# Context's feed-forward in a hybrid retention trunk: from a planned loop to a list of units in a fixed order

## The chip, the cores and the metric

The kernel runs on one core of one Trainium2 chip. The metric is device time in microseconds (us) for one execution. The core has five instruction queues: TensorE (PE, matmuls; its weight loads are listed as PEld), VectorE (DVE), ScalarE (ACT), GpSimd (POOL) and SyncE (SP), which here issues nearly all DMAs. Each queue runs its instructions in order.

## The reference

One layer of a diffusion backbone: 1024 latent tokens and 256 context tokens of width 1024 pass through the same weights. Cut to what matters here:

```python
def swiglu(h, w1, w3, w2):
    return (jax.nn.silu(h @ w1) * (h @ w3)) @ w2

x = x + 0.5 * m_l[2] * swiglu(modulate(rms_norm(x, norm1_w), m_l[0], m_l[1]), ffn1_w1, ffn1_w3, ffn1_w2)
ctx = ctx + 0.5 * m_c[2] * swiglu(modulate(rms_norm(ctx, norm1_w), m_c[0], m_c[1]), ffn1_w1, ffn1_w3, ffn1_w2)
y_l, _ = token_mixing(modulate(rms_norm(x, norm2_w), m_l[3], m_l[4]),
                      modulate(rms_norm(ctx, norm2_w), m_c[3], m_c[4]), w_in, ...)
x = x + m_l[5] * y_l
x = x + 0.5 * m_l[8] * swiglu(modulate(rms_norm(x, norm3_w), m_l[6], m_l[7]), ffn2_w1, ffn2_w3, ffn2_w2)
return rms_norm(x, final_norm_w)
```

The hidden width is 2816, that is 22 blocks of 128 (f = 0 to 21). The change concerns the second of these lines: the first feed-forward, for the 256 context tokens.

## The kernel before

Everything is float32, and activations lie transposed: 128 features on the partitions, tokens along the free axis. A product of two float32 matrices is made of three fast matmuls (mm3, L63). Each operand is split (L58) into a high part, a rounded copy made by ACT, and a low part, the remainder, made by a subtraction on DVE or POOL. A weight block of 128 x 1024 is loaded and split as two halves of 128 x 512.

Token groups are numbered 0 and 1 (512 latent tokens each) and 2 (the context). The latent feed-forward is arranged as seven block products in place of eight (chain, L302, for w1 and w3; back6, L493, and prod, L466, for w2). back6 works off products 1, 2, 6, 5, 7 and 3, each in eleven pairs p; product 4 follows later. After each pair a feeder (L550) runs what stands at that place of `plan`, a table from the pair's number to small tasks: loads, steps of norms and the like. Products keep four PSUM banks "psa" or four "psb"; there are eight banks in all.

After back6 comes the context's feed-forward (L1575):

```python
for f in range(0, NF, 2):
    self.classic(f, (2,), mid2=(lambda: self.Y(f - 2, CT)) if f else None, ...)
    pend.pop(0)()
```

`classic` (L621) loads and splits w1 and w3 for blocks f and f+1, the low parts on POOL. H (L616) multiplies one weight block with the normed context into a psa bank: 24 matmuls of 256 columns. s1 (L578) takes the SiLU on ACT. s3 (L584) multiplies on DVE and splits the result into ghi (ACT) and glo (DVE). Y (L591) then multiplies the blocks f-2 and f-1 with w2: for each of the eight 128-row pieces m of the output, six matmuls into a fresh psb bank, and one DVE instruction (L600) that adds the scaled sum onto x. So x is updated 88 times over the eleven pairs. The last Y (f = 20) stands in `plan` after the second pair of product 4.

Between the pairs, `pend` runs the second norm of latent group 1 step by step: the rest of the sum of squares (norm2(1, 0), ahead of the loop), the row factor (L181, L197), eight steps norm_k (L226: two DVE instructions, one on ACT), and the spill of x to HBM. Then follow product 4, the norm of group 0, the context's key and value projections (ctx_k, ctx_v), mix_setup with lg_setup (L840: log-sigmoid of eight decay values by a row of tiny DVE instructions and one POOL power), and the mixing stage.

The order on each engine is set by a planner. It takes instructions by program order, moved by priorities: loading and splitting of weights are put 150 places ahead (WPRI), or, where POOL makes the low part, at their own place (WOFF). Raw loads use six buffers "raw" (NR), splits six pairs "whi"/"wlo" (NH), or slots of the activations' tiles that are free at the time (hslot). A block under `manual_schedule` keeps program order on the engines that it names; other work may still be put between. back6 is in such a block for SP alone. The context's loop is in none.

Of the kernel before, what the change touches and what calls it, by code (L numbers as in the profile page):

```python
# [31 lines left out]
class Trunk:  # L32
# [224 lines left out]
    def raw_half(self, src=None):  # L257
        t = self.tile(self.wp, [P, 512], F32, "raw", NR)
        if src is not None:
            t = t[:, :src.shape[1]]  # L260
            self.nc.sync.dma_start(t, src)
        return t
# [7 lines left out]
    def load_half(self, src, dst=None, eng=None):  # L270
        with self.tc.high_priority(offset=WOFF if eng else WPRI):
            return self.half(self.raw_half(src), dst, eng)

    def halves_slots(self, i):
        if i < 2:
            return None, None
        return tuple(self.hslot(f"0{2 * (i % 4) + j}") for j in range(2))

    def load_halves(self, src, dst=(None, None), eng=None):
        return [self.load_half(src[:, 512 * i:512 * i + 512], dst[i], eng) for i in range(2)]  # L280
# [310 lines left out]
    def Y(self, f, order, after=None, qs=(0, 1)):  # L591
# [18 lines left out]
        if after:  # L610
            for tg, o, n in order:
                for m in range(KD):
                    unit(ws[m // 4], tg, o, n, m)
                after(tg, o, n)

    def H(self, w, tg):  # L616
        ps = self.psA()
        self.proj(w, tg, ps)
        return ps
# [217 lines left out]
            act(a, a, AF.Exp, scale=-1.0)  # L837
            act(a, a, AF.Ln, bias=1.0)

    def lg_setup(self):  # L840
        nc, I, cp = self.nc, self.I, self.cp2
        x = self.tile(cp, [P, 8], F32, "lgx")
        nc.sync.dma_start(x, I["decay"].broadcast_to([P, 8]))
        e = self.tile(cp, [P, 8], F32, "lge")
        nc.vector.memset(e, float(np.e))
        u = self.tile(cp, [P, 8], F32, "lgu")
        nc.vector.tensor_scalar(out=u, in0=x, scalar1=-1.0, scalar2=None, op0=ALU.mult)
        nc.vector.tensor_tensor(out=u, in0=u, in1=x, op=ALU.min)
        nc.gpsimd.tensor_tensor(out=u, in0=e, in1=u, op=ALU.pow)
# [11 lines left out]
        nc.vector.scalar_tensor_tensor(out=x, in0=e, scalar=-2.0, in1=x, op0=ALU.mult, op1=ALU.add)  # L861
        self.lg = x
# [581 lines left out]
    def run(self):  # L1444
        nc, tc, I = self.nc, self.tc, self.I
        S = {}

        def opn(name, side="left"):
            S[name] = tc.tile_pool(name=name, bufs=1, reuse_waits="tile", side=side)
            return S[name].__enter__()  # L1450

        def cls(name):
            S[name].__exit__(None, None, None)
# [19 lines left out]
        with tc.manual_schedule(engines={mybir.EngineType.PE, mybir.EngineType.DVE, mybir.EngineType.Activation}):  # L1473
            ws = self.first1((xp, xp, None), n1)
# [24 lines left out]
        hc = opn("hc", "right")  # L1499
        self.gp = hc  # L1500
        n2 = opn("n2", "right")
        self.alloc_h((2,), hc)
# [32 lines left out]
        norm2 = lambda tg, i: norm_step(tg, i, self.mcol(4, int(tg == 2)), self.mcol(3, int(tg == 2)))  # L1535
        for i, at in enumerate((24, 27, 30, *range(33, 33 + KD))):
            plan[at].append(lambda i=i: ctx1(i))

        CT = [(2, 0, 256)]
        p4 = 6 * NP  # L1540
        plan[p4 + 1] += [lambda: self.Y(NF - 2, CT), lambda: self.alloc_h((2,), hc), lambda: norm2(2, 0)]
        plan[p4 + 4].append(lambda: norm2(2, 1))
        plan[p4 + 6].append(lambda: norm2(2, 2))
        for k in range(KD):
# [27 lines left out]
        self.alloc_h((1,), self.hp)  # L1572
        norm2(1, 0)
        pend = [lambda i=i: norm2(1, i) for i in range(1, 3 + KD)] + [lambda: spill(1)]
        for f in range(0, NF, 2):  # L1575
            self.classic(f, (2,), mid2=(lambda: self.Y(f - 2, CT)) if f else None, eng=[nc.gpsimd if e else None for e in CENG])
            pend.pop(0)()
        A = self.bank4(self.psA)
        self.prod(4, A, True)
        self.add4(0, 1, A)  # L1580
# [7 lines left out]
            norm2(0, 3 + k)  # L1588
        spill(0)
        cls("n2"), cls("hc"), cls("xp")  # L1590
        self.cp2 = opn("cp2", "right")
        self.mix_setup()
        cls("f1")
# [52 lines left out]
NLOW = 150  # L1646
SH = 2
NR = 6
EMODS = ((5, (0,)), (2, (0, 1)), (1, (1,)), (0, (1,)), (4, (0, 1)), (3, (0, 1)), (7, (0,)), (6, (0,)))
MPER = 6  # L1650
NH = 6
# [14 lines left out]
CENG = (1, 1, 1, 1)  # L1666
# [98 lines left out]
```

## Time and profile before

| | us |
|---|---|
| median of 3 runs | 2174.63 (2174.54 to 2177.96) |
| profiled execution | 2173.67 |
| span of its trace, first to last instruction | 2171.8 |
| PE busy | 2113.6 (97%) |
| DVE busy | 1525.9 (70%) |
| ACT busy | 979.9 (45%) |
| POOL busy | 279.9 (13%) |

Times in the trace count from the first instruction. A row of a group names the line, the engine, the operation, output and inputs, their shapes and the count, then busy time and mean duration, then the idle time of that engine just ahead of those instructions and who ended it. A line may be that of a helper: L60 and L61 are the two halves of every split, L65 to L67 the three matmuls of every mm3. A matmul's listed duration is longer than the distance to the next one, since matmuls overlap; the distance between starts is its cost. In rows of stretches the two numbers after the granted clock are the busy share of the DMA engines and GB/s.

### The profile page before, as it was taken

How to read it: one execution, taken by the hardware profiler on the slowest of the kernel's cores; microseconds unless marked ns; L12 is line 12 of the kernel's file. 1: busy time of each engine (PE TensorE's matmuls, PEld its weight loads, DVE VectorE, ACT ScalarE, POOL GpSimd, SP SyncE). 2: the span in 40 equal slices, each digit the busy share in tenths (PEclk: the TensorE clock that was granted, in tenths of full speed). 3: DMA queues.
4: the chain of work that ended last, by engine and by line, in shares of the span. 5: the costliest groups of instructions: out<-in, count | busy, mean ns of one | idle time of the engine just before them, and what ended most of it. 6: DMA issues, size and time to landing. Idle time of an engine off the chain costs nothing. (4 is left out here: it accounts for less than half of the span.)

```text
span 2171.8 us, 32819 instructions
## 1 busy us (share of the span) xinstructions
PE 2113.6 (97%) x11558; PEld 1806.7 (83%) x11558; DVE 1525.9 (70%) x2735; ACT 979.9 (45%) x1811; POOL 279.9 (13%) x285
## 2 busy tenths in 40 slices
PE   8999999999999899999989999999999999999998
PEld 7888888888889899987778987787878888888888
DVE  7889999756766756844666556858777666665686
ACT  4434334345545444547455335524343433434553
POOL 0000000000025662611132113200000000010000
PEclk9999999999999999999999999999999999999999
DMA  9267768569966565653322322324144444467674
GB/s 332 83 232 242 268 222 272 168 221 328 305 201 191 161 183 172 179 155 103 94 67 62 99 55 90 121 93 155 61 129 160 139 157 160 155 213 248 212 243 146
DMA packets 202933, 373.39 MB, mean 172 GB/s; under 512 B 24016, under 2 KB 37264, under 8 KB 202768
## 3 DMA queue, kind: packets, MB, share of 16 engines
q1 hardware_dynamic: 202336, 371.16, 52.9%
q8 instruction: 90, 1.47, 0.3%
q14 instruction: 75, 0.61, 0.1%
q10 hardware_dynamic: 432, 0.13, 0.0%
HBM read 296.72 MB, written 66.09 MB: 167 GB/s over the span
## 5 line engine op out<-in xcount | busy, mean ns | idle before, releaser
L60 ACT ACTIVATE whi<-raw 128x512 fp32r<-128x512 f32 (+1 forms) x563 | 346.9, 622 | 615.7 <-PE psa L66 181.1
L61 DVE TENSOR_TENSOR wlo<-raw,whi 128x512 fp32r<-128x512 f32 (+1 forms) x533 | 369.3, 696 | 309.0 <-ACT whi L60 304.6
L65 PE MATMUL psa<-hh,whi 128*128 128x512 f32 (+1 forms) x1108 | 434.4, 392 | 0.1
L66 PE MATMUL psa<-hl,whi 128*128 128x512 f32 (+1 forms) x1108 | 433.8, 391 | 0.0
L67 PE MATMUL psa<-hh,wlo 128*128 128x512 f32 (+1 forms) x1108 | 433.5, 391 | 0.0
L65 PE MATMUL psb<-hh,whi 128*128 128x512 f32 (+1 forms) x680 | 259.8, 382 | 0.5 <-ACT whi L60 0.5
L67 PE MATMUL psb<-hh,wlo 128*128 128x512 f32 (+1 forms) x680 | 259.7, 382 | 0.6 <-DVE wlo L61 0.6
L66 PE MATMUL psb<-hl,whi 128*128 128x512 f32 (+1 forms) x680 | 259.5, 382 | 0.0
L65 PEld LDWEIGHTS psa<-hh,whi 128*128 128x128 f32 x1108 | 208.7, 188 | 42.1 <-ACT s L314 0.6
L67 PEld LDWEIGHTS psa<-hh,wlo 128*128 128x128 f32 x1108 | 208.6, 188 | 41.6
L66 PEld LDWEIGHTS psa<-hl,whi 128*128 128x128 f32 x1108 | 208.6, 188 | 40.9
L67 PEld LDWEIGHTS psb<-hh,wlo 128*128 128x128 f32 x680 | 127.8, 188 | 25.8 <-DVE wlo L61 1.0
L65 PEld LDWEIGHTS psb<-hh,whi 128*128 128x128 f32 x680 | 127.9, 188 | 25.4 <-ACT whi L60 1.0
L66 PEld LDWEIGHTS psb<-hl,whi 128*128 128x128 f32 x680 | 127.9, 188 | 24.6
L60 ACT ACTIVATE hh<-raw 128x512 fp32r<-128x512 f32 x180 | 110.3, 622 | 72.6 <-PE psa L66 38.2
L61 POOL TENSOR_TENSOR hl<-raw,hh 128x512 fp32r<-128x512 f32 x84 | 117.5, 1410 | 67.2 <-ACT hh L60 62.6
L1095 POOL TENSOR_TENSOR nr<-nr,mhalf 128x4 f32<-128x4 f32 (+1 forms) x11 | 10.6, 963 | 867.5 <-DVE nr L1094 867.5
L65 PE MATMUL psa<-hh,hh 128*128 128x256 f32 x376 | 107.5, 286 | 1.2 <-DVE s L587 1.2
L67 PE MATMUL psa<-hh,hl 128*128 128x256 f32 x376 | 107.5, 286 | 0.0
L66 PE MATMUL psa<-hl,hh 128*128 128x256 f32 x376 | 107.4, 286 | 0.0
L65 PE MATMUL psa<-whi,hh 128*128 128x256 f32 (+1 forms) x320 | 93.3, 292 | 1.2 <-ACT s L1049 1.2
L66 PE MATMUL psa<-wlo,hh 128*128 128x256 f32 (+1 forms) x320 | 93.2, 291 | 1.0 <-DVE wlo L61 0.9
(402 smaller groups left out, 4238.2 us busy)
## 6 DMA issues: line engine op xcount, KB each, us to landing
raw<-in_w SPq DMA_DIRECT2D x374, 256.0 KB, 3.2
gd<-s SPq DMA_DIRECT2D x154, 256.0 KB, 2.8
ada<-in_adaT SPq DMA_DIRECT2D x76, 512.0 KB, 4.8
raw<-gd SPq DMA_DIRECT2D x91, 256.0 KB, 3.4
s<-in_w SPq DMA_DIRECT2D x66, 256.0 KB, 4.7
sd<-s SPq DMA_DIRECT2D x44, 256.0 KB, 3.1
raw<-sd SPq DMA_DIRECT2D x44, 256.0 KB, 2.9
hh<-in_w SPq DMA_DIRECT2D x44, 256.0 KB, 3.9
```

Of the source, the lines that this page charges most:

```text
L60: nc.scalar.activation(hi, src, AF.Copy)
L61: (eng or nc.vector).tensor_tensor(out=lo, in0=src, in1=hi.bitcast(F32), op=ALU.subtract)
L65: mm(ps, wa[0], xa[0], start=start, stop=False, skip_group_check=more)
L66: mm(ps, wa[0], xa[1], start=False, stop=False, skip_group_check=more)
L67: mm(ps, wa[1], xa[0], start=False, stop=stop, skip_group_check=more)
L1095: nc.gpsimd.tensor_tensor(out=r, in0=r, in1=self.mhalf[:, :n], op=ALU.pow)
```

## The change

The loop becomes a list of units: ("1", f) and ("3", f) for w1 and w3 of a block, ("y", f) for w2 of blocks f and f+1. The order is 1 0, 3 0, 1 1, 3 1, 1 2, 3 2, y 0, 1 3, 3 3, 1 4, 3 4, y 2 and so on. ctx_ffn walks the list under `manual_schedule` for all five queues. At each unit it issues the load of the unit five places on (CLA); at a "1" or "3" it also issues the split of the "1" or "3" two places on among these, and one of the four halves of the next y, then the matmuls, then s1 or s3. The w2 sums of all blocks stay in four psb banks, two pieces m to a bank, and x is updated eight times after the last y, which stands at the same place of `plan` as before.

Raw weights are loaded into the pool "s" (19 buffers, also used for the latent stream's kept sums) in place of "raw". The first five units are loaded after pairs 3 to 7 of product 3 and the first two split after pairs 8 and 9. The norm of group 1 takes its steps one by one behind the y units (its banks now psa, its four diagonal tiles made at once), and each of its result tiles is allocated when its step comes. lg_setup is cut in two: lg_start (the log-sigmoid) stands right behind the block, ahead of product 4.

```diff
+    def ctx_sums(self, f, ws):
+        for m in range(KD):
+            ps = self.yb[m // 2][:, m % 2 * CTX:(m % 2 + 1) * CTX]
+            for i in range(2):
+                self.mm3(ps, [t[:, m % 4 * P:(m % 4 + 1) * P] for t in ws[2 * (m // 4) + i]], self.g[f + i, 2],
+                         not (f or i or m % 2), f == NF - 2 and i == 1, True)
+            if f == NF - 2:
+                x = self.x[2][m]
+                self.nc.vector.scalar_tensor_tensor(out=x, in0=ps, scalar=self.gates_m[1][:, m:m + 1], in1=x,
+                                                    op0=ALU.mult, op1=ALU.add)
...
+    def ctx_load(self, u):
+        self.craw[u] = []
+        for src in self.ctx_src(u):
+            t = self.stile()
+            self.nc.sync.dma_start(t, src)
+            self.craw[u].append(t)
+        self.cw[u] = []
...
+    def ctx_hsplit(self, u):
+        j = 2 * u[1] + (u[0] == "3")
+        for i in range(2):
+            slot = f"1{(self.ng // 2 + 5 + 2 * j + i) % 8}" if j < 4 else f"0{2 * (j % 4) + i}"
+            self.ctx_split(u, self.hslot(slot), self.nc.gpsimd)
+
+    def ctx_ffn(self, units, norms):
+        self.yb = self.bank4(self.psB)
+        hs = [u for u in units if u[0] != "y"]
+        ys = [u for u in units if u[0] == "y"]
+        j = 0
+        for i, u in enumerate(units):
+            for v in units[i + CLA:i + CLA + 1]:
+                self.ctx_load(v)
+            if u[0] != "y":
+                j += 1
+                for v in hs[j + 1:j + 2]:
+                    self.ctx_hsplit(v)
+                for v in ys[:1]:
+                    if v in self.cw and len(self.cw[v]) < 4:
+                        self.ctx_split(v)
+                ps = self.H(self.cw.pop(u), 2)
+                (self.s1 if u[0] == "1" else self.s3)(u[1], 2, ps)
+            else:
+                self.ctx_sums(u[1], self.cw.pop(u))
+                ys.pop(0)
+                if norms:
+                    norms.pop(0)()
...
-        CT = [(2, 0, 256)]
         p4 = 6 * NP
-        plan[p4 + 1] += [lambda: self.Y(NF - 2, CT), lambda: self.alloc_h((2,), hc), lambda: norm2(2, 0)]
+        units = []
+        for f in range(0, NF, 2):
+            units += [("1", f), ("3", f)] + ([("y", f - 2)] if f else []) + [("1", f + 1), ("3", f + 1)]
+        self.craw, self.cw = {}, {}
+        for i in range(CLA):
+            plan[5 * NP + 3 + i].append(lambda u=units[i]: self.ctx_load(u))
+        for i in range(2):
+            plan[5 * NP + 8 + i].append(lambda u=units[i]: self.ctx_hsplit(u))
+        last = ("y", NF - 2)
+        plan[p4 + 1] += [lambda: self.ctx_sums(NF - 2, self.cw.pop(last)), lambda: self.alloc_h((2,), hc), lambda: norm2(2, 0)]
...
-        pend = [lambda i=i: norm2(1, i) for i in range(1, 3 + KD)] + [lambda: spill(1)]
-        for f in range(0, NF, 2):
-            self.classic(f, (2,), mid2=(lambda: self.Y(f - 2, CT)) if f else None, eng=[nc.gpsimd if e else None for e in CENG])
-            pend.pop(0)()
...
+        norms = [lambda: norm2(1, 1), diag1, rows1] + [lambda k=k: norm1(k) for k in range(KD - 1)]
+        with tc.manual_schedule(engines={mybir.EngineType.PE, mybir.EngineType.DVE, mybir.EngineType.Activation,
+                                         mybir.EngineType.Pool, mybir.EngineType.SP}):
+            self.ctx_ffn(units, norms)
+            self.ctx_load(last)
+        for _ in range(4):
+            self.ctx_split(last)
+        norm1(KD - 1)
+        spill(1)
+        self.lg_start(n2)
+        self.psN = self.psB
```

More of the change, by code (lines that the diff above doesn't have):

```diff
@@ L272, in load_half @@
             return self.half(self.raw_half(src), dst, eng)
[L274 to L277, printed above, removed]
     def load_halves(self, src, dst=(None, None), eng=None):
@@ new lines, in ctx_src @@
+    def ctx_src(self, u):
+        kind, f = u
+        if kind == "y":
+            return [self.w2[f + i][:, 512 * q:512 * q + 512] for q in range(2) for i in range(2)]
+        return [(self.w1 if kind == "1" else self.w3)[f][:, 512 * i:512 * i + 512] for i in range(2)]
+    def ctx_load(self, u):
[5 more added lines that the diff above has]
+        self.cw[u] = []
@@ new lines, in ctx_split @@
+    def ctx_split(self, u, dst=None, eng=None):
+        src = self.craw[u][len(self.cw[u])]
+        self.cw[u].append(self.half(src, dst, eng))
+    def ctx_hsplit(self, u):
[25 more added lines that the diff above has]
+                    norms.pop(0)()
@@ L838, in softplus, with lg_start @@
             act(a, a, AF.Ln, bias=1.0)
-    def lg_setup(self):
-        nc, I, cp = self.nc, self.I, self.cp2
+    def lg_start(self, cp):
+        nc, I = self.nc, self.I
         x = self.tile(cp, [P, 8], F32, "lgx")
@@ L860, in lg_setup @@
         nc.vector.tensor_scalar(out=x, in0=x, scalar1=0.0, scalar2=None, op0=ALU.min)
-        nc.vector.scalar_tensor_tensor(out=x, in0=e, scalar=-2.0, in1=x, op0=ALU.mult, op1=ALU.add)
-        self.lg = x
+        self.lg = self.mcol(0, 1)
+        nc.vector.scalar_tensor_tensor(out=self.lg, in0=e, scalar=-2.0, in1=x, op0=ALU.mult, op1=ALU.add)
+    def lg_setup(self):
+        nc, cp, x = self.nc, self.cp2, self.lg
         self.kd = {}
@@ L1501, in run @@
         n2 = opn("n2", "right")
+        self.ndg = 4
         self.alloc_h((2,), hc)
@@ L1570, in spill, with norm1, diag1, rows1 @@
                 nc.sync.dma_start(self.xd[k * P:(k + 1) * P, o:o + 512], self.x[tg][k])
-        self.alloc_h((1,), self.hp)
+        self.h[1] = []
         norm2(1, 0)
-        pend = [lambda i=i: norm2(1, i) for i in range(1, 3 + KD)] + [lambda: spill(1)]
-        for f in range(0, NF, 2):
-            self.classic(f, (2,), mid2=(lambda: self.Y(f - 2, CT)) if f else None, eng=[nc.gpsimd if e else None for e in CENG])
-            pend.pop(0)()
+        def norm1(k):
+            self.h[1].append(self.hslot(f"1{k}"))
+            norm2(1, 3 + k)
+        self.psN = self.psA
+        def diag1():
+            dg.extend(self.rows_diag(nrm[1], b, n2) for b in range(4))
+        def rows1():
+            pr = self.rstd_rows(nrm[1], 512, n2, None, dg)
+            nrm[1] = self.scr(n2, "nrb")
+            nc.scalar.copy(nrm[1], pr)
+        dg = []
+        norms = [lambda: norm2(1, 1), diag1, rows1] + [lambda k=k: norm1(k) for k in range(KD - 1)]
[9 more added lines that the diff above has]
+        self.psN = self.psB
         A = self.bank4(self.psA)
@@ L1590, in run @@
         cls("n2"), cls("hc"), cls("xp")
+        self.ndg = 2
         self.cp2 = opn("cp2", "right")
@@ L1648 @@
 NR = 6
+CLA = 5
 EMODS = ((5, (0,)), (2, (0, 1)), (1, (1,)), (0, (1,)), (4, (0, 1)), (3, (0, 1)), (7, (0,)), (6, (0,)))
```

## The prediction

> **What bounds the kernel now.** First the page: its totals.
>
> ```profile
> span 2171.8 us, 32819 instructions
> PE 2113.6 (97%) x11558; PEld 1806.7 (83%) x11558; DVE 1525.9 (70%) x2735; ACT 979.9 (45%) x1811; POOL 279.9 (13%) x285
> ```
>
> TensorE (PE) is busy in 97% of the span, so a change that leaves the number of matmuls alone can win only where PE waits or runs slowly. The second view, the instructions of the line with the SiLU of this feed-forward, puts the context's stage between 645 and 862 us. The third, busy time by stretch (length, then busy us and count for each engine, granted clock, share of the DMA engines, GB/s), cuts that stage in two:
>
> ```profile
> 630.00:645.25 15.25, 15.25 (x69) 12.64 (x68) 8.48 (x14) 9.05 (x16) 8.04 (x6) 1.00 0.22 63
> 645.25:736.00 90.75, 80.64 (x634) 79.19 (x634) 65.65 (x99) 46.09 (x87) 56.71 (x40) 0.96 0.58 177
> 736.00:850.00 114.00, 114.00 (x938) 113.35 (x937) 58.03 (x110) 53.75 (x102) 59.04 (x44) 1.00 0.59 180
> 760.00:800.00 40.00, 40.00 (x336) 40.00 (x335) 19.64 (x35) 20.35 (x39) 25.09 (x20) 1.00 0.60 182
> ```
>
> The last row gives the pitch of a 256-column matmul when nothing is late: 40.00 / 336 = 0.119 us. At that pitch the 634 matmuls of the first stretch need 75.4 us; they took 90.75. **So 15.3 us can be won in the first half, and nothing in the second**, where PE never pauses although the order is still the planner's. Fourth, who made PE wait between 645 and 862 us (total us, times, longest):
>
> ```profile
> PE psb L65 <- DVE x L600: 8.5, 4, 3.6
> PE psa L65 <- DVE s L587: 1.2, 1, 1.2
> PE psb L66 <- DVE glo L61: 0.3, 1, 0.3
> ```
>
> These are 10.0 us, which is the 90.75 - 80.64 = 10.1 of PE's idle time. The other 5.2 us of the 15.3 are matmuls that came slowly after a wait. Fifth, four short stretches show that:
>
> ```profile
> 672.00:678.00 6.00, 3.14 (x24) 2.94 (x24) 3.27 (x8) 3.21 (x6) 4.90 (x5) 1.00 0.62 205
> 678.00:682.00 4.00, 3.91 (x18) 3.92 (x19) 2.66 (x6) 0.00 (x0) 1.05 (x2) 0.51 0.71 223
> 682.00:686.00 4.00, 4.00 (x25) 4.00 (x24) 2.84 (x5) 2.19 (x4) 2.36 (x3) 0.64 0.24 81
> 710.00:716.00 6.00, 2.38 (x20) 2.17 (x19) 6.00 (x10) 2.57 (x6) 2.66 (x2) 1.00 0.48 140
> ```
>
> After 2.9 idle us of 6.00, the granted clock was 0.51 and then 0.64: 43 matmuls in 8.00 us where the pitch asks 5.1, some 2.9 us lost. [...] Sixth, the timeline at that longest pause (start, length, engine, instruction):
>
> ```profile
> 711.46 0.41 DVE L587 TENSOR_TENSOR s<-psa,s 128x256 f32<-128x256 f32 x1
> 711.79 1.42 DVE L223 SCALAR_TENSOR_TENSOR hl<-nt,modl,hh 128x512 fp32r<-128x512 f32 x1
> 713.47 1.25 DVE L600 SCALAR_TENSOR_TENSOR x<-psb,modc,x 128x256 f32<-128x256 f32 x3
> 714.00 0.39 PE L65 MATMUL psb<-ghi,whi 128*128 128x256 f32 x1 [3.62 <-DVE x L600]
> ```
>
> VectorE (DVE) was never idle there. It did norm steps of the latent stream, which the planner had piled up here, before the updates of x that would have freed PSUM banks. PE waited on the order of DVE's queue, not on its load.
>
> **The change, part by part.** Matmuls and their shapes stay: a unit "1" or "3" is 24 matmuls (2.86 us at 0.119), a unit "y" 48 (5.71), so a pair of f is 17.1 us. The other engines' instructions in this stage:
>
> ```profile
> L61 POOL TENSOR_TENSOR hl<-raw,hh 128x512 fp32r<-128x512 f32 x79 | 110.6, 1412 | 67.1 <-ACT hh L60 62.6 <-PE psb L67 1.1
> L60 ACT ACTIVATE hh<-raw 128x512 fp32r<-128x512 f32 x84 | 51.7, 625 | 58.6 <-PE psa L66 38.2 <-issue 11.6 <-DMA raw<-gd 3.0
> L61 DVE TENSOR_TENSOR wlo<-raw,whi 128x512 fp32r<-128x512 f32 x52 | 41.5, 808 | 41.5 <-ACT whi L60 41.4
> L600 DVE SCALAR_TENSOR_TENSOR x<-psb,modc,x 128x256 f32<-128x256 f32 x88 | 38.5, 473 | 1.1 <-PE psb L67 1.0
> L61 DVE TENSOR_TENSOR glo<-s,ghi 128x256 fp32r<-128x256 f32 x22 | 16.6, 757 | 5.8 <-ACT ghi L60 5.3
> L217 DVE SCALAR_TENSOR_TENSOR nt<-x,modl,nrb 128x512 f32<-128x512 f32 x8 | 9.4, 1187 | 0.8 <-ACT nrb L1530 0.6
> L587 DVE TENSOR_TENSOR s<-psa,s 128x256 f32<-128x256 f32 x22 | 9.2, 419 | 32.5 <-PE psa L67 32.3 <-ACT s L581 0.2
> L60 ACT ACTIVATE ghi<-s 128x256 fp32r<-128x256 f32 x22 | 9.1, 415 | 9.4 <-DVE s L587 9.4
> L581 ACT ACTIVATE s<-psa 128x256 f32<-128x256 f32 x22 | 8.1, 366 | 1.9 <-PE psa L67 1.9
> L218 ACT ACTIVATE hh<-nt,modl 128x512 fp32r<-128x512 f32 x8 | 5.8, 723 | 7.6 <-DVE nt L217 7.6
> ```
>
> 1. *Sums in PSUM.* 80 of the 88 updates of x go: 80 x 0.473 = 37.8 us of DVE. In the second half they hid under PE entirely. What counts is that no w2 unit waits for a bank any more: 8.5 us of waits, and the slow matmuls behind them.
>
> 2. *Fixed order.* Work of a pair by the rows above: ScalarE (ACT) 12 x 0.625 + 2 x 0.366 + 2 x 0.415 + 0.723 = 9.8 us; DVE 4 x 0.808 + 2 x 0.419 + 2 x 0.757 + 2 x 1.187 = 8.0; GpSimd (POOL) 8 x 1.412 = 11.3, all under 17.1. New waits in order: ACT's SiLU now stands behind the splits two units ahead, and those splits stand behind the SiLU or ghi of the unit before, which waits for PE. That chain, from the end of a unit on PE: product 0.42, ghi 0.42, hi 0.63, lo on POOL 1.41 = 2.9 us to the first half, 4.3 to the second. PE asks for the first after two units, 5.7 us, and for the second 1.4 later. Slack 2.8 us: cost nothing, covered by the unit between. DVE's product stands behind one lo of w2, which waits for ACT's third split; walked through, it comes 0.2 us late in a quartet and the 5.7 us of y take that back. A norm step (0.72 on ACT, 2.4 on DVE) starts in y too and ends inside it. I put 1.2 + 0.3 us of the other waits at nothing as well.
>
> 3. *Loads five units ahead.* The same 132 loads of 256 KB, from SyncE's queue (SP), into 19 buffers in place of six. Its waits from 600 to 860 us, the loads' time to landing, and the first context loads of before:
>
> ```profile
> SPq L261 <- POOL hl L61: 103.5, 82, 4.2
> raw<-in_w SPq DMA_DIRECT2D x135, 256.0 KB, 3.1
> 638.94 15.29 SPq L261 DMA_DIRECT2D raw<-in_w  x13
> ```
>
> SP waited 103.5 us for POOL to free one of the six. Five units hold at most 12 buffers, the sums kept from the latent stream 4, SiLU results 2: 18 of 19, so loads go out 10 us or more before use, against 3.1 to land. The first ten now stand among the last loads of the latent stream's product; the DMA engines were 0.22 busy in 630 to 645 us, so nothing is late for it. Cost 0.
>
> 4. *Seam at the start.* The norm's four squares stand before the block. They need the last updates of x:
>
> ```profile
> 651.36 2.48 DVE L481 TENSOR_TENSOR s<-psb,s 128x512 f32<-128x512 f32 x4
> 653.75 2.73 DVE L487 SCALAR_TENSOR_TENSOR x<-s,modl,x 128x512 f32<-128x512 f32 x4
> ```
>
> If ACT had to run the squares first, the third unit's splits would start 5.2 + 0.6 us after 645.3, and their lo end 0.6 + 1.4 later: 7.8, where PE asks after 5.7, so 2.1 us, and some 1 more for the next unit. If the planner fits the ready splits in ahead, as it did in before, 0. Ends 0 and 3; I take 0, since PE crossed this seam without a pause.
>
> 5. *Seam at the end.* The last w2 unit is split after the block, and product 4's first pair must be split inside it. ACT has no splits of its own left in the last two units, so there is room; ends 0 and, if pair 0 is loaded and split only after the block, 3.1 + 0.63 + 0.81 = 4.5. The last sums update x one half bank at a time while PE writes the other half: four pauses of 0 to 0.473, so 0 to 1.9. [...] For the first I take 0, since product 4 follows in before without a pause; for the second half of 1.9, since product 4's matmuls can fill some of the pauses: 1.0 for the whole seam.
>
> 6. *lg_start moved.* About 25 tiny DVE instructions, one on POOL and one load leave this place:
>
> ```profile
> 929.17 0.17 DVE L847 TENSOR_SCALAR lgu<-lgx 128x8 f32<-128x8 f32 x1 [2.48 <-DMA lgx<-in_decay]
> 929.63 1.78 POOL L849 TENSOR_TENSOR lgu<-lge,lgu 128x8 f32<-128x8 f32 x1 [4.83 <-DVE lgu L848]
> 934.16 0.40 PE L66 MATMUL psa<-wlo,hh 128*128 128x288 f32 x1 [0.59 <-DVE wlo L61]
> ```
>
> The one pause of PE beside them is 0.59 us: a gain of 0 to 0.6. Where they go, product 4, DVE could be made late by as much; I take 0, ends -0.6 and 0.6. The later stages are planned anew; I allow 2 us either way and take 0.
>
> Sum: 15.3 - 1.0 = **14.3 us gained**. The profiled execution took 2173.67 us (span 2171.8 and 1.9 around it), 1.0 below the median 2174.63 of the three runs; 2173.67 - 14.3 = 2159.4, as a median **2160.3 us**.
>
> **Rivals.** *The seams eat half.* Items 4 and 5 at their far ends: 3 + 4.5 + 1.9 = 9.4, so 5.9 gained, 2168.7. For it: ACT, DVE, POOL and SP are all pinned through the block, and only unpinned work can slip in. Against it: the planner had no pause at either seam before.
>
> *Slower: the list runs at ACT's and POOL's pace.* Every split of a w1 or w3 half now waits in ACT's queue behind a SiLU or ghi that waits for PE. If PE then waits for the splits, each unit pays again, 44 times. POOL's splits are the loose part:
>
> ```profile
> L61 POOL TENSOR_TENSOR hl<-raw,hh x79: 1268/1298/2437, 649.6 to 829.9; 128x512 fp32r<-128x512 f32 x79
> ```
>
> At the median or mean POOL has room; at the longest, 2.437 each, a pair needs 8 x 2.437 = 19.5 us against PE's 17.1, 2.4 x 11 = 26 us, and the time would be 2174.6 - 14.3 + 26 = 2186. It decides at (15.3 + 11 x 17.1) / 88 = 2.3 us a split.
>
> *No change.* PE's pauses were only moved: the norm steps, product and splits trade places, and PE pauses as long elsewhere: 2174.6. The gapless second half speaks against it.
>
> **How the numbers follow.** Forecast (12 to 18 gained) 0.57, its own range 2156.5 to 2162.5; seams (4.3 to 12 gained) 0.22; no change 0.06; list too slow 0.15. A gain of 18 takes 15.3, 0.6 and the 2 us of replanning. 0.2% is 4.3 us, about what a measurement tells from no change. A loss needs more than 4.3 us, and the slow list has it. So faster 0.79, same 0.06, slower 0.15. The range 2155 to 2171 holds the forecast and nearly all of the seams' case.
>
> **What would show it.** Right: 645 to 736 us' work shows PE at 0.119 us a matmul, no wait for x, granted clock 1.00, DVE's updates of x in this line 8, and SP waiting less for POOL. Step 4 or 5 wrong: a pause of PE beside the squares or at product 4's first pairs. Wrong altogether: PE waiting for POOL's lo or ACT's hi in units again and again, or pauses of several us in the stages after 900 us that the planner laid anew.

## The result and the profile after

Over six runs each the kernel with the list takes 2165.22 us (median, 2159.39 to 2169.0) and the kernel before 2177.99 (2174.54 to 2182.23). The ratio is 0.9942, 95% interval 0.9924 to 0.9960: 12.8 us gained. The time lies within the range of 2155 to 2171. The forecast of 2160.3 is 4.9 too low, mainly because the kernel before, over six runs, has a median 3.4 us above that of the three runs shown; the gain itself was forecast as 14.3.

The profiled execution took 2167.51 us. The head of its page:

```profile
span 2165.7 us, 32720 instructions
PE 2113.8 (98%) x11558; PEld 1805.7 (83%) x11558; DVE 1497.1 (69%) x2655; ACT 975.8 (45%) x1811; POOL 289.8 (13%) x285
```

The same matmuls (11558), 80 DVE instructions fewer, and a PE that is as busy as before in a shorter span. Now the context's stage, cut as in the prediction. It runs from PE's first 256-column matmul of the context to the end of the last product with a SiLU (columns: the stretch, its length, busy us and count of each engine, granted clock, share of the DMA engines, GB/s):

```profile
648.22:739.22 91.00, 91.00 (x758) 90.70 (x757) 41.69 (x60) 44.59 (x90) 63.59 (x43) 1.00 0.65 215
739.22:835.42 96.20, 96.11 (x801) 95.91 (x800) 44.03 (x60) 48.14 (x94) 60.47 (x40) 1.00 0.45 148
```

In its first 91 us PE does 758 matmuls at 0.120 us, where before it did 634 in 90.75, and the clock stays at 1.00. The whole stage takes 187.20 us; by the same marks it took 201.72 before. Who made PE wait between 640 and 862 us (total, times, longest) is a single row, and it belongs to the last w2 unit, behind the block:

```profile
PE psb L67 <- DVE wlo L61: 0.7, 1, 0.7
```

The groups that answer to the prediction's rows, from 646 to 862 us (busy, mean ns of one, then idle time ahead):

```profile
L61 POOL TENSOR_TENSOR hl<-s,hh 128x512 fp32r<-128x512 f32 x82 | 122.7, 1523 | 60.9 <-ACT hh L60 59.0 <-PE psa L67 1.9
L61 DVE TENSOR_TENSOR wlo<-s,whi 128x512 fp32r<-128x512 f32 x44 | 41.9, 954 | 76.3 <-ACT whi L60 73.1 <-DMA s<-in_w 3.1
L217 DVE SCALAR_TENSOR_TENSOR nt<-x,modl,nrb 128x512 f32<-128x512 f32 x8 | 5.8, 740 | 0.0
L619 DVE SCALAR_TENSOR_TENSOR x<-psb,modc,x 128x256 f32<-128x256 f32 x8 | 3.6, 476 | 0.0
```

88 updates of x (38.5 us) have become eight (3.6). DVE now idles 76 us ahead of w2's low halves, since in a fixed order it stands and waits for ACT's high half; PE does not notice.

The whole span fell by 6.1 us only, though the stage gave 14.5. The rest, from the marks in the two traces: the stage starts 3.0 later (648.2 against 645.3), the piece from its end to the first copy of the context's keys takes 1.6 more (43.8 against 42.2), the mixing after that 3.7 more (518.9 against 515.2), and what follows 0.2 more: -14.5 + 3.0 + 1.6 + 3.7 + 0.2 = -6.0. PE's instructions stand in the same order in both kernels up to the stage and from about 930 us on, so the 3.0 and the 3.7 are not work that the change moved on PE. To see what is spread, both kernels ran once more as they are.

### The profile page after: what moved, and what is told of

The parts are those of the page before. It is cut to its first block, busy times and chain, and to the rows that moved or that the text cites. A ratio compares the mean times of both kernels' runs of the same rounds, so it can differ in the third digit from the quotient of the medians.

```text
span 2165.7 us, 32720 instructions
## 1 busy us (share of the span) xinstructions
PE 2113.8 (98%) x11558; PEld 1805.7 (83%) x11558; DVE 1497.1 (69%) x2655; ACT 975.8 (45%) x1811; POOL 289.8 (13%) x285
## 3 DMA queue, kind: packets, MB, share of 16 engines
q8 instruction: 90, 1.47, 0.3%
## 5 line engine op out<-in xcount | busy, mean ns | idle before, releaser
L60 ACT ACTIVATE whi<-raw 128x512 fp32r<-128x512 f32 (+1 forms) x515 | 318.4, 622 | 607.4 <-PE psa L66 179.0
L61 DVE TENSOR_TENSOR wlo<-raw,whi 128x512 fp32r<-128x512 f32 (+1 forms) x489 | 334.6, 687 | 283.1 <-ACT whi L60 277.6
L65 PE MATMUL psa<-hh,whi 128*128 128x512 f32 x1092 | 431.1, 395 | 0.4 <-ACT s L309 0.3
L66 PE MATMUL psa<-hl,whi 128*128 128x512 f32 x1092 | 430.6, 394 | 0.0
L67 PE MATMUL psa<-hh,wlo 128*128 128x512 f32 x1092 | 430.2, 394 | 0.0
L66 PE MATMUL psb<-hl,whi 128*128 128x512 f32 (+1 forms) x680 | 259.5, 382 | 0.0
L66 PEld LDWEIGHTS psa<-hl,whi 128*128 128x128 f32 x1092 | 206.4, 189 | 41.0
L61 POOL TENSOR_TENSOR hl<-s,hh 128x512 fp32r<-128x512 f32 x88 | 131.9, 1525 | 144.1 <-ACT hh L60 139.3
L66 PEld LDWEIGHTS psb<-hl,whi 128*128 128x128 f32 x680 | 127.9, 188 | 24.5
L66 PE MATMUL psa<-hl,hh 128*128 128x256 f32 x392 | 110.9, 283 | 0.0
L61 DVE TENSOR_TENSOR wlo<-s,whi 128x512 fp32r<-128x512 f32 x44 | 41.9, 954 | 76.3 <-ACT whi L60 73.1
L66 PE MATMUL psa<-wlo,hh 128*128 128x256 f32 (+1 forms) x320 | 92.6, 289 | 0.1
L67 PE MATMUL psa<-whi,hl 128*128 128x256 f32 (+1 forms) x320 | 92.4, 289 | 0.0
```

The source lines that it names most:

```text
L60: nc.scalar.activation(hi, src, AF.Copy)
L61: (eng or nc.vector).tensor_tensor(out=lo, in0=src, in1=hi.bitcast(F32), op=ALU.subtract)
L65: mm(ps, wa[0], xa[0], start=start, stop=False, skip_group_check=more)
L66: mm(ps, wa[0], xa[1], start=False, stop=False, skip_group_check=more)
L67: mm(ps, wa[1], xa[0], start=False, stop=stop, skip_group_check=more)
```

## The experiments

The theory of the forecast, A in the expectations, was that PE waits for banks because updates of x stand behind norm steps on DVE, and that sums kept in PSUM end it. Its rivals, B and C, were that the weights' loads and splits come too late, and that the planner's order of the queues is the fault, so that the fixed order carries the gain. Each part of the change was then done alone on the kernel before or undone on the kernel after. One table holds all of it: the start of the stage, its length, PE's matmuls in its first 91 us, the piece from its end to the first ctx_k copy, the median time, and the ratio to the kernel before in the same comparison.

| kernel | start | stage | matmuls in 91 us | to ctx_k | median us | ratio [95%] |
|---|---|---|---|---|---|---|
| before | 645.3 | 201.72 | 637 | 42.2 | 2177.99 | |
| b2: before again | 646.1 | 198.98 | 660 | 42.3 | 2178.37 | 1.0001 [0.9990, 1.0011] |
| after | 648.2 | 187.20 | 758 | 43.8 | 2165.22 | 0.9942 [0.9924, 0.9960] |
| a2: after again | 646.7 | 187.18 | 758 | 43.8 | 2163.93 | 0.9927 [0.9908, 0.9947] |
| e_psum: before, sums in PSUM | 647.4 | 194.95 | 693 | 42.5 | 2171.87 | 0.9977 [0.9965, 0.9989] |
| e_buf: before, 19 load buffers | 647.4 | 273.36 | 479 | 41.8 | 2250.84 | 1.0337 [1.0319, 1.0354] |
| e_norm: before, norm steps later | 647.5 | 206.73 | 694 | 42.3 | 2182.85 | 1.0025 [1.0013, 1.0037] |
| e_order: after, 88 updates of x | 646.9 | 190.74 | 758 | 43.1 | 2168.76 | 0.9963 [0.9949, 0.9977] |
| e_plan: after, only SP fixed | 646.4 | 188.49 | 747 | 43.8 | 2166.89 | 0.9948 [0.9933, 0.9963] |
| e_free: after, no queue fixed | 646.8 | 187.30 | 756 | 43.9 | 2162.73 | 0.9930 [0.9913, 0.9946] |
| e_jit: after, splits one unit ahead | 646.2 | 195.06 | 711 | 44.0 | 2170.94 | 0.9968 [0.9955, 0.9982] |
| e_pool: after, w2's low halves on POOL | 646.2 | 204.62 | 707 | 43.9 | 2182.35 | 1.0021 [1.0010, 1.0032] |
| e_last: after, last w2 load in the list | 646.3 | 187.23 | 758 | 42.5 | 2163.20 | 0.9933 [0.9910, 0.9955] |
| e_lg: after, lg_setup whole again | 648.1 | 187.14 | 758 | 44.0 | 2164.36 | 0.9939 [0.9922, 0.9955] |

The 3.0 us at the start are within the spread: it begins at 645.3 to 648.2 in all these traces, at 648.2 and 646.7 in the two of after, and at 647.5 in e_norm, whose edit lies behind that point. So are the 3.7 of the mixing stage: 515.2 and 518.5 us in the two traces of before, 518.9 and 516.4 in the two of after. The stage's own length is the sharper measure, and the text below goes by it.

### The sums alone

```diff
         def unit(w, tg, o, n, m):
-            ps = self.psB()
+            ps = self.yb[m // 2][:, m % 2 * CTX:(m % 2 + 1) * CTX]
...
+            if f < NF - 2:
+                return
             x = self.x[tg][m][:, o:o + n]
...
+        self.yb = self.bank4(self.psB)
+        self.psN = self.psA
```

> The kernel before with one part of the change alone: the w2 sums stay in four PSUM banks and x is updated eight times at the end; the loop, its buffers and the planner's order stay. The stage is counted from PE's first 256-column matmul of the context to the end of the last product with the SiLU; it took 201.7 us before and 187 after. Theory A (PE waited for updates of x that stood in VectorE's queue behind piled-up norm steps): no wait for x is left, stage 188 to 192, total 10 to 13 us under the kernel before. Theory B (weights come late because six raw buffers are too few): stage 199 to 202, total unchanged. Theory C (only the fixed order of all queues helps): stage 196 to 201, since norm steps then hold up products and low halves in place of updates.

The stage takes 194.95 us. No wait for x is left, so that part of the forecast's reading holds, but only 4.0 to 6.8 us of the stage are won (from 198.98 and 201.72). That lies between what theory A (188 to 192) and theory C (196 to 201) had expected. PE's two long waits in this kernel, then the instructions around the first of them (start, length, engine, line; the bracket is the idle time before and who ended it):

```profile
PE psb L65 <- ACT ghi L60: 3.0, 1, 3.0
PE psa L203 <- DVE ndiag L194: 1.0, 1, 1.0
```

```profile
651.30 0.69 DVE L61 TENSOR_TENSOR wlo<-raw,whi 128x512 fp32r<-128x512 f32 x1 [11.34 <-ACT whi L60]
...
660.56 0.68 DVE L178 TENSOR_TENSOR nacc<-nacc,nsq 128x512 f32<-128x512 f32 x1
661.16 0.42 DVE L587 TENSOR_TENSOR s<-psa,s 128x256 f32<-128x256 f32 x1
661.62 0.42 ACT L60 ACTIVATE ghi<-s 128x256 fp32r<-128x256 f32 x1 [1.59 <-DVE s L587]
662.08 0.58 PE L65 MATMUL psb<-ghi,whi 128*128 128x256 f32 x1 [3.04 <-ACT ghi L60]
```

The planner had put a low half of w2 at the head of DVE's queue before its high half was there. DVE stood 11.3 us, everything behind it came late, the product of the SiLU last, and PE waited 3.0 us for it. It then ran slowly: 18 matmuls in the four us from 663 to 667, at a granted clock of 0.50, where 33 fit. What was late was data. ACT's waits for the raw weights from 645 to 836 us, in before and then in this kernel:

```profile
ACT whi L60 <- DMA raw<-in_w: 13.8, 11, 3.7
```

```profile
ACT whi L60 <- DMA raw<-in_w: 33.7, 19, 4.5
```

In after the same wait is 1.3 us in the same stretch. So with the waits for x gone, the late loads were next.

### The list without the sums

```diff
-            ps = self.yb[m // 2][:, m % 2 * CTX:(m % 2 + 1) * CTX]
+            ps = self.psB()[:, :CTX]
...
-            if f == NF - 2:
-                x = self.x[2][m]
-                self.nc.vector.scalar_tensor_tensor(out=x, in0=ps, scalar=self.gates_m[1][:, m:m + 1], in1=x,
-                                                    op0=ALU.mult, op1=ALU.add)
+            x = self.x[2][m]
+            self.nc.vector.scalar_tensor_tensor(out=x, in0=ps, scalar=self.gates_m[1][:, m:m + 1], in1=x,
+                                                op0=ALU.mult, op1=ALU.add)
```

> The kernel after without the sums in PSUM: the list, its loads and the fixed order of all queues stay, but every w2 unit takes eight fresh sums in four psb banks and x is updated 88 times. VectorE then has 8.0 + 8 x 0.473 = 11.8 us a pair against PE's 17.1. Theory A (order, not load): stage 187 to 190, total as after. If the sums in PSUM are what counts under any order: PE waits for banks in the w2 units, stage 193 or more, total 6 us or more above after. Theory B: as A, since the loads are early.

190.74 us, with all 88 updates of x in place, and one pause, at the end:

```profile
646.88:837.62 190.74, 187.57 (x1559) 187.11 (x1558) 118.62 (x199) 91.81 (x184) 126.01 (x83) 1.00 0.56 177
```

```profile
825.33 2.02 DVE L61 TENSOR_TENSOR hl<-raw,hh 128x512 fp32r<-128x512 f32 x2
827.27 0.41 DVE L61 TENSOR_TENSOR glo<-s,ghi 128x256 fp32r<-128x256 f32 x1
827.61 2.09 DVE L618 SCALAR_TENSOR_TENSOR x<-psb,modc,x 128x256 f32<-128x256 f32 x5
828.23 0.36 PE L65 MATMUL psb<-ghi,whi 128*128 128x256 f32 x1 [3.16 <-DVE x L618]
```

DVE is busy 118.6 of 190.7 us, so 80 more instructions are no load problem. The pause has the form that the prediction showed at 714 us: other work (here the low halves of product 4) ahead of the updates of x. Together with the run before this makes a table of four: neither part 199.0 to 201.7, the sums 195.0, the list 190.7, both 187.2. The sums give 4.0 to 6.8 alone and 3.5 on top of the list; the list gives 8.2 to 11.0 alone and 7.8 on top of the sums. The list is the larger part. It stands here for all of the change but the sums: the units' order, the loads, their buffers, the splits and the new places of the norm's steps.

### Which part of the list

*The fixed order.* First all queues but SP were given back to the planner, then SP too.

```diff
-        with tc.manual_schedule(engines={mybir.EngineType.PE, mybir.EngineType.DVE, mybir.EngineType.Activation,
-                                         mybir.EngineType.Pool, mybir.EngineType.SP}):
+        with tc.manual_schedule(engines={mybir.EngineType.SP}):
             self.ctx_ffn(units, norms)
```

> The kernel after with the fixed order for SP alone: list, loads five units ahead and sums in PSUM stay, but the planner orders PE, VectorE, ScalarE and GpSimd in the context's stage. Theory A (without updates of x the planner's order is good enough): stage 187 to 191, total within 4 us of after. Theory C (the fixed order is what counts): stage 195 or more, total 6 us or more above after.

```diff
-        with tc.manual_schedule(engines={mybir.EngineType.PE, mybir.EngineType.DVE, mybir.EngineType.Activation,
-                                         mybir.EngineType.Pool, mybir.EngineType.SP}):
+        if True:
             self.ctx_ffn(units, norms)
```

> The kernel after with no fixed order on any queue in the context's stage, SP among them: the list's program order, the 19 buffers, the loads five units and the splits two units ahead and the sums in PSUM are left, all under the planner. With SP alone fixed the stage took 188.5 us. If SP's fixed order is what keeps the weights early: the planner brings loads forward or holds them, stage 195 or more. If the early emission of loads and splits is enough: stage 187 to 190, total within 4 us of after.

188.49 and 187.30 us. The window of e_free's stage:

```profile
646.82:834.12 187.30, 187.22 (x1557) 186.61 (x1555) 87.70 (x119) 92.48 (x179) 109.39 (x81) 1.00 0.55 181
```

PE is busy 187.22 of 187.30 us with no queue in a fixed order. The order set by hand on five queues is worth nothing that these runs can measure, once loads and splits are issued early in the program, in a pool that holds them, and the sums stay in PSUM.

*The lead of the splits.* w1 and w3 are split one unit ahead instead of two; the loads stay five ahead.

```diff
-                for v in hs[j + 1:j + 2]:
+                for v in hs[j:j + 1]:
...
-        for i in range(2):
+        for i in range(1):
             plan[5 * NP + 8 + i].append(lambda u=units[i]: self.ctx_hsplit(u))
```

> The kernel after with the splits of w1 and w3 one unit ahead in place of two, the loads as they are. From the end of a unit on PE the first half is ready 0.37 + 0.62 + 1.5 = 2.5 us later behind a SiLU, and 0.42 + 0.42 + 0.62 + 1.5 = 3.0 behind a product, the second 1.5 after it; PE asks after 2.86 and 4.29. If this chain is right: no pause behind a SiLU, 0.3 to 0.5 us behind half of the products, where no w2 unit covers, so 3 to 6 us in all: stage 190 to 194. If each unit pays a whole round trip, as the kernel with 19 buffers under the planner did: 40 units by 0.8 us or more, stage 220 or more.

195.06 us, 7.9 more. PE's waits in this kernel:

```profile
PE psa L67 <- POOL hl L61: 1.1, 2, 0.9
PE psa L65 <- ACT hh L60: 1.0, 1, 1.0
```

The start costs 4.1 us (the first w2 unit begins 21.8 us into the stage, against 17.7 in after), more than the expectation had, and each pair then 0.3 to 0.7, mostly 0.4, in pauses too short for most of them to be listed as waits. So the second unit of lead is needed; taken away it costs about what the list adds to the sums (7.8). No run took back the loads' lead alone or the norm's new places, so how the list's gain divides among these and the splits' lead is not shown.

*The buffers.* The raw weights of the loop go into the 19 buffers of "s", with the loop of before.

```diff
-        t = self.tile(self.wp, [P, 512], F32, "raw", NR)
+        t = self.stile() if self.wide else self.tile(self.wp, [P, 512], F32, "raw", NR)
...
+        self.wide = True
         for f in range(0, NF, 2):
...
+        self.wide = False
```

> The kernel before with the raw weights of this stage in the 19 buffers of pool s in place of six, nothing else. Theory A: stage 199 to 203, total within 3 us of before. Theory B: stage 188 to 192, total 10 to 13 us less. Theory C: as A.

The stage takes 273.36 us, 72 more than before; no theory had that. The edit shifts the lines by one (L61 and L62 are the halves of a split here, L66 to L68 the matmuls, L582 the SiLU). The waits of the stage, and one turn of what repeats:

```profile
PE psa L66 <- ACT hh L61: 25.5, 21, 3.3
PE psa L68 <- POOL hl L62: 18.7, 22, 1.2
ACT s L582 <- PE psa L68: 83.4, 20, 7.6
```

```profile
767.12 0.38 ACT L582 ACTIVATE s<-psa 128x256 f32<-128x256 f32 x1 [7.17 <-PE psa L68]
767.40 2.18 ACT L61 ACTIVATE hh<-s 128x512 fp32r<-128x512 f32 x4
768.10 5.03 POOL L62 TENSOR_TENSOR hl<-s,hh 128x512 fp32r<-128x512 f32 x4 [6.64 <-ACT hh L61]
```

The planner now puts the splits of the next weights behind the SiLU of the blocks before. ACT waits 7.2 us for PE, then splits, and PE waits for that split: a round trip per block. This is the mechanism of the slower rival, ACT's splits behind a SiLU that waits for PE, with another order. Why more buffers make the planner order so (the SiLU's results share this pool with the loads) was not tried and stays open. It shows that early loads alone are no gain: without splits that stand early in the program the wide pool does harm.

### Are the norm steps what piles up on DVE?

The kernel before, with the norm's steps from pair 5 on, two a pair:

```diff
         for f in range(0, NF, 2):
...
-            pend.pop(0)()
+            for _ in range(min(len(pend), 2 if f >= 10 else 0)):
+                pend.pop(0)()
```

> The kernel before with the steps of latent group 1's norm taken from pair 5 on, two for each pair, in place of one for each pair from the first. Theory A: the first 91 us of the stage lose under 5 us in place of 15.3, and some pauses for x appear in the second half where the norm now is: stage 190 to 197. Theory B: the first half pauses as before, 10 us or more, whatever the norm does: stage 200 to 203. Theory C: pauses only move, stage 199 to 204.

206.73 us, more than any of the three theories had (204 at most). The two parts of the stage and PE's waits:

```profile
647.49:738.49 91.00, 86.41 (x694) 85.80 (x693) 47.60 (x84) 44.79 (x85) 56.99 (x43) 0.96 0.63 192
738.49:854.22 115.73, 108.32 (x864) 107.18 (x863) 72.40 (x122) 53.36 (x101) 56.23 (x41) 0.96 0.55 163
```

```profile
PE psb L65 <- DVE x L600: 7.6, 4, 4.0
PE psb L203 <- DVE ndiag L194: 3.7, 1, 3.7
```

The first 91 us lose 8.4 us instead of 15.2 (694 matmuls, not 637, at 0.119), and the second part, which had lost nothing, now loses 12.9 (115.73 for 864). Where the norm now is, PE waits 3.7 us for the norm's diagonal tiles, and 2.0 and 0.7 us, at 789 and 791 us, for updates of x behind norm steps. But the longest wait for x, 4.0 us, lies in the first half, where the loop has no norm step left. It stands behind low halves of w2, for the first of which DVE had waited for ACT's high half, as ACT had waited 3.6 us for its load:

```profile
669.75 0.69 DVE L61 TENSOR_TENSOR wlo<-raw,whi 128x512 fp32r<-128x512 f32 x1 [3.54 <-ACT whi L60]
672.90 0.58 PE L65 MATMUL psb<-ghi,whi 128*128 128x256 f32 x1 [3.98 <-DVE x L600]
```

In before, two of the four waits for x, 1.25 us at 672.8 and 2.17 at 678.1, stand likewise behind a low half for which DVE had waited. The second of them:

```profile
676.72 0.92 DVE L61 TENSOR_TENSOR wlo<-raw,whi 128x512 fp32r<-128x512 f32 x1 [2.43 <-ACT whi L60]
678.09 0.58 PE L65 MATMUL psb<-ghi,whi 128*128 128x256 f32 x1 [2.17 <-DVE x L600]
```

The last wait for x in before (1.47 us at 733.5) stands behind two low halves as well. Norm steps stood ahead of the longest alone, 3.6 of the 8.5 us. So they are one part of what delayed the updates, and spreading them over other pairs moves their pauses and adds to them; the low halves of w2 are the other part.

### How near POOL is to being the bound

The kernel after, with w2's four low halves a pair on POOL instead of DVE, twelve low halves in place of eight:

```diff
-                        self.ctx_split(v)
+                        self.ctx_split(v, None, self.nc.gpsimd)
```

> The kernel after with the low halves of w2 (four for each pair) moved from VectorE to GpSimd. GpSimd's splits took 1.525 us each in the kernel after, so a pair needs 12 x 1.525 = 18.3 us of it against PE's 17.1. If the pace of GpSimd sets the list as soon as it is over PE's (the slower rival's mechanism): stage 187 + 10 x 1.2 = 197 to 201, PE waiting for hl or wlo of GpSimd, total 9 to 13 us above after. If splits two units ahead hide it: stage 187 to 190.

```profile
646.20:850.82 204.62, 191.02 (x1557) 188.59 (x1555) 67.25 (x79) 92.31 (x184) 165.30 (x123) 0.99 0.53 165
```

```profile
PE psb L67 <- POOL wlo L61: 13.4, 9, 2.6
```

17.4 us lost, more than expected, though POOL is busy only 165.3 of 204.6 us: its splits took 1.39 us, not the 1.525 that the expectation was worked out from, and twelve make 16.7, under PE's 17.1 a pair. POOL is not at its rate; the fourth low half of each w2 unit is late for its date, and PE waits up to 2.6 us at nearly every one. The slower rival was right that POOL is the loose part. Its turning point of "2.3 us a split" is a sum of throughput, and this run shows that such a sum is not enough: here a due time is missed with POOL a fifth idle.

### The end of the block, lg_start, and the spread

In after, the one wait of PE (0.7 us, at 836 us) stands in the last w2 unit. SP's queue says why. Its issues from 802 to 832 us (L632 is the block's load, L261 that of product 4):

```profile
801.94 1.52 SPq L632 DMA_DIRECT2D s<-in_w  x2
822.67 0.33 SPq L261 DMA_DIRECT2D raw<-gd  x1
826.08 0.33 SPq L261 DMA_DIRECT2D raw<-in_w  x1
827.01 0.33 SPq L261 DMA_DIRECT2D raw<-gd  x1
827.62 0.33 SPq L261 DMA_DIRECT2D raw<-in_w  x1
828.04 1.81 SPq L632 DMA_DIRECT2D s<-in_w  x4
```

The planner put four loads of product 4 ahead of the last w2 unit's load. The first of them waited for a "raw" buffer, the queue stood from 803 to 823 us, and the last w2 load went out at 828, for use at 835. In e_last that load is part of the list:

```diff
-            for v in units[i + CLA:i + CLA + 1]:
+            for v in (units + [("y", NF - 2)])[i + CLA:i + CLA + 1]:
                 self.ctx_load(v)
...
-            self.ctx_load(last)
```

> The kernel after with the load of the last w2 unit inside the list, five units ahead like the others, in place of behind it. In the kernel after this load went out 6 us before its use and PE paused 1.2 us at the last w2 unit. If SyncE's queue, blocked by loads of product 4 that the planner had put ahead, made it late: that pause is under 0.3 us and the time to the end of product 4 falls by 1 us. If not: the pause stays. The total can show either only within its own spread of 4 us.

```profile
792.31 13.92 SPq L632 DMA_DIRECT2D s<-in_w  x11
820.77 0.33 SPq L261 DMA_DIRECT2D raw<-gd  x1
```

That wait is gone, and the piece to the first ctx_k copy falls from 43.8 to 42.5 us, as in before. The total, 2163.20, cannot be told from the 2163.93 of after on the same chip. By its trace this is the best version found; by its time it equals after.

For e_lg the call goes back into lg_setup:

```diff
+        self.lg_start(self.cp2)
...
-        self.lg_start(n2)
```

> The kernel after with lg_start back at the head of lg_setup, in the mixing stage's set-up. By the prediction it is worth 0 to 0.6 us: the context's stage stays at 187.2, and from its end to the first output of the mixing stage the time is the same within 1 us plus the spread of 1 us seen between two traces of the kernel after.

With lg_setup whole again the stage takes 187.14 us, and from its end to the first output of mixing it is 243.1, against 243.2 and 241.5 in the two traces of after. The move is worth nothing that these traces can tell.

The two kernels as they are:

> The kernel after, unchanged, to see how far two traces of the same program lie apart by stage. In the first trace the context's stage began 2.9 us later than before and 4 us were lost between 1110 and 1260 us, though the queues hold the same instructions in the same order on PE up to the stage and from 930 us on. If these are spread of the chip: they come out differently here, by 1 us or more, and the context's stage itself repeats within 0.5 us of 187. If the change caused them: they repeat.

> The kernel before, unchanged, for a second trace. If the pauses in the first half of the context's stage belong to the program's order: the stage takes 201.7 us within 1.5, and PE waits for updates of x at the same w2 units. If they were an accident of one execution: it is shorter or the pauses lie elsewhere. The beginning of the stage and the mixing stage may differ by 3 to 6 us, as they did between two traces of the kernel after's program.

The stage of after repeats to 0.02 us. That of before is 198.98 in the second trace, 2.7 less than in the first where 1.5 had been allowed; its first part has the same four waits for x, shorter in sum (7.4 us):

```profile
646.14:737.14 91.00, 83.32 (x660) 82.09 (x659) 66.95 (x103) 46.65 (x88) 54.51 (x39) 0.96 0.58 181
737.14:845.12 107.98, 107.98 (x900) 107.85 (x899) 54.89 (x103) 51.66 (x99) 58.98 (x44) 1.00 0.59 183
```

The stage's gain is thus 11.8 to 14.5 us. Less the 1.5 at the end seam that is 10.3 to 13.0, and the medians say 12.8.

## Why the prediction was right, by its steps

- *15.3 us in the first half, nothing in the second.* Right. PE is now busy 91.00 of 91.00 us there, at the pitch read from the gapless stretch; the second half was at that pitch already. In b2 what could be won is 12.5 (91.00 - 660 x 0.119).
- *Step 1, the sums.* Right in part. The waits for x and the slow matmuls behind them do go, but the step gave them the whole gain, and alone it wins 4.0 to 6.8 us. That norm steps stand ahead of the updates was read from the longest pause and holds for 3.6 of the 8.5 us. The other waits stood behind low halves of w2, two of them held up by late high halves, and with the updates gone such a low half held DVE's queue, and PE with it. That the total fits all the same is in part luck: the step counted everything that PE lost as its own, and the list, which was given no gain, removed the rest.
- *Step 2, the fixed order.* Cost nothing, as said. It also brings nothing: the planner reaches 187.30 us from the same list. The chain with 2.8 us of slack is real: with one unit of lead PE loses 7.9 us.
- *Step 3, the loads.* Cost 0 is right. The step looked only for what it could cost, though the list, of which early loads and splits are a part, carries the larger half of the gain. That SP would wait much less for POOL was a poor sign to look for: from 600 to 860 us it waits 92.6 us for it, against 103.5, but now several units ahead of the need.

```profile
SPq L632 <- POOL hl L61: 92.6, 59, 6.1
```

- *Step 4, seam at the start.* 0, right: no pause of PE there.
- *Step 5, seam at the end.* 1.0 forecast, 1.3 to 1.6 measured, for another reason: neither the splits of product 4 nor the shared banks, but the last w2 load behind blocked loads in SP's queue. No run shows the 1.9 us of the prediction's estimate for the last updates of x (four pauses of 0.473, half of them in the 1.0): in after the eight updates (837.5 to 852.8 us) came while PE worked on product 4 or on other sums, and PE listed no wait for them.
- *Step 6, lg_start.* 0, right, but it did not go where the step put it: its load was issued at 456.6 us and its DVE work ran from 459.8 to 476.7, but for one instruction at 570, all in the latent feed-forward.
- *The 2 us for what is planned anew.* Too small, and misnamed: from 930 us on PE's order is the same, and still the mixing stage differs by 3.7 us, and by 3.3 between two traces of before. That is spread between executions; single runs of after lie 9.6 us apart.
- *The forecast's own range, 2156.5 to 2162.5,* missed by 2.7 us: 3.4 of it is the level of before, taken from three runs, and 1.5 the smaller gain (12.8 for 14.3).
- *The rivals.* Seams that eat half: no, 1.5 us. Moved pauses: not in after, but e_norm shows that this does happen in this stage when the norm alone is moved. The slow list: not in after; e_pool and e_buf show it, at 17 and 72 us.

## What to carry to other kernels

When PE waits behind another engine's queue, find the instruction at that queue's head and what it waits for, remove it in thought, and ask again: here the waits for x (8.5 us in before) hid late weights of nearly the same price (e_psum, without those waits, is still 7.8 us above after). The list issued early in the program, with its lead on loads and splits, did what the order by hand was meant to do (a stage of 187.30 us with no queue fixed, 187.20 with all five); try the lead first and fix the order only where a trace still shows a blocked head. A bound by throughput was not enough for an engine that feeds PE in bursts (e_pool lost 17.4 us with POOL busy 165.3 of 204.6): work out when the last piece of each burst is due.

## What the runs showed of the hardware

DVE and POOL slowed each other where both worked on pairs of SBUF tensors: an instruction of DVE went from 0.74 us to 1.78, a split of POOL from 1.30 (median) to 2.44. The updates of x, which read a PSUM bank, kept 0.466 to 0.485 us in all 88 cases of before, with POOL splitting or not. The norm's instruction on DVE (line and engine as before; count, then shortest, median and longest ns, and the span of starts) in before, then in after, then in e_pool:

```profile
L217 DVE SCALAR_TENSOR_TENSOR nt<-x,modl,nrb x8: 735/1086/1780, 702.6 to 725.7; 128x512 f32<-128x512 f32 x8
```

```profile
L217 DVE SCALAR_TENSOR_TENSOR nt<-x,modl,nrb x8: 737/739/743, 721.7 to 828.5; 128x512 f32<-128x512 f32 x8
```

```profile
L217 DVE SCALAR_TENSOR_TENSOR nt<-x,modl,nrb x6: 1776/1780/1781, 722.3 to 817.7; 128x512 f32<-128x512 f32 x6
```

It takes 0.74 us where POOL happens to be idle and up to 1.78 where POOL was already splitting, and POOL's splits go from 1.28 at the least to 1.52 on average in after. In one place of before (719 us) two of these DVE instructions kept their 0.74 us, and the split of POOL that began just behind the first took 2.44. The 1.04 us added at most to the DVE instruction is less than one split of POOL, 1.28 at the least. Why the two engines hold each other up is not shown.

In these traces the clock after a pause is not settled by the pause's length. The longest pause of before, 3.62 us, comes in b2 at the same instructions and lasts 3.68:

```profile
711.67 0.39 PE L65 MATMUL psb<-ghi,whi 128*128 128x256 f32 x1 [3.68 <-DVE x L600]
```

The four us behind it, in before and then in b2:

```profile
714.00:718.00 4.00, 4.00 (x33) 4.00 (x34) 4.00 (x9) 0.72 (x1) 0.00 (x0) 1.00 0.17 57
```

```profile
712.00:716.00 4.00, 4.00 (x25) 4.00 (x24) 3.84 (x9) 0.72 (x1) 0.00 (x0) 0.64 0.19 45
```

33 matmuls at a clock of 1.00 against 25 at 0.64: the same program pays about 1 us (8 x 0.119) in one execution and nothing in the other. Nor is there a bound between 3.62 and 3.68: in e_pool a pause of 2.34 us, which ended at 840.6, was followed by matmuls 0.214 us apart (841.51 to 844.72), and one of 2.62, which ended at 726.9, by matmuls 0.12 apart (727.16 to 731). What settles the clock is not shown.
